# Norm rows from products with ones, smaller first pieces, earlier weight requests and five state buffers in a hybrid recurrent step

## The chip, the cores and the metric

The kernel runs on one core of one Trainium2 chip. A core has a matrix engine (TensorE, PE in the profile; its weight loads are PEld), a vector engine (VectorE, DVE), an engine for functions of one operand (ScalarE, ACT), a general one (GpSimd, POOL) and a queue engine (SyncE, SP) that here only issues transfers. Each engine works through its own instructions in order and waits on semaphores for the others. The metric is the time of one launch in microseconds on the device; lower is better. Kernels are compared by the median of several launches.

## The reference

One step of a two-layer decoder trunk runs over 256 prompt tokens and 8 x 8 sample tokens, 320 rows of 2048 columns, all in float32. Layer 0 mixes a gated delta rule (8 heads of 128x128 state) with gated linear attention (4 heads of 128x256 state); layer 1 is a gated linear recurrence (RG-LRU). What matters here are the norms, the four large products and the states:

```python
def _rmsnorm(x, g):
    xf = x.astype(jnp.float32)
    y = xf * lax.rsqrt(jnp.mean(xf * xf, axis=-1, keepdims=True) + EPS)
    return (y * g.astype(jnp.float32)).astype(x.dtype)

for l in range(DEPTH):                       # DEPTH = 2
    if l % 2 == 0:
        h = _rmsnorm(x, ab_norm[j])
        y, sa, ca, sb = _ab_mixer(h, ...)    # einsum with w_in, conv, delta rule, GLA, einsum with w_out
    else:
        h = _rmsnorm(x, lru_norm[j])
        y, hl, cl = _lru_mixer(h, ...)       # einsum with w_in, conv, gates, scan, einsum with w_out
    x = x + y
return (_rmsnorm(x, final_norm), ...)        # and all new states
```

For the sample tokens every sequence brings its own states (8 x 8 delta matrices, 8 x 4 GLA matrices), which are read, updated and written back.

## The kernel before

**Layout.** Activations lie with the 2048 columns on partitions, 16 tiles of 128 x 320 (tokens on the free axis). A dense product is made in "groups" of 512 output columns, 30 in all: 14 for the input projection of layer 0, 4 for its output, 8 for the input of layer 1, 4 for its output. A group runs over 8 "chunks" of weights (two blocks of 128 x 512, 512 KB). Float32 accuracy comes from splitting both operands into a high and a low part, so each pair of blocks takes three products (line 242): high x high, high weights x low x, low weights x high x. A chunk thus has 2 x 4 x 3 = 24 products of 320 columns, and the kernel has 5760 of them. A group accumulates in four PSUM banks (`accs`, four buffers), so the next group's first product needs the first bank of the group before to have been read.

**Weights.** `load_chunk` (line 197) asks for a chunk on the SP queue into one of three buffers `wst`. `split_chunk` (line 210) makes the high part `wh` on ACT (line 216) and the low part `wl` on DVE (line 219), six half-chunk buffers each. While chunk i is multiplied, chunk i+2 is split (`ahead`, line 224), and at the start of chunk i chunk i+3 is asked for (line 235). The first chunk is special: its halves are asked for by SP and ACT at once (lines 207, 208 and 1599), and the first half is cast on DVE (line 218).

**The order of the rest.** All other work is written as Python generators in three queues, `hi`, `lo` and `tails`. After each half of a chunk's quarter, `slot` advances each queue by one `yield`; there are eight slots per chunk. A table `WAITS` says how many yields a generator lets pass at each place. The framework then orders each engine's instructions by priority (the order in which they are emitted, with offsets for the splits and evictions) and by when their inputs are ready, so an instruction emitted late can run early. `behind` ties one to the product emitted last. When a queue runs late, `finish`, `until` and `drain` empty it on the spot.

**First norm row (r0).** `tables` (line 1658) loads x a second time, with tokens on partitions (`xtok`, 2.6 MB in eight transfers). `start_work` (line 1671) makes the sums of squares from it: two DVE instructions and one ACT instruction for each of four column blocks. `row_rstd` (line 311) scales them, takes the power -1/2 on POOL (line 279), and `spread_rows` (line 303) turns the column into a row on all partitions with three products against the identity (line 307); DVE copies it into `rb0` (line 318). `rb0` multiplies the results of the first layer's groups. Group 0's raw results are put into the buffer `slab` by ACT (lines 421, 422) and scaled later in `taps` (line 430), followed by the convolution (lines 434 to 437). There is one `slab`; group 1's eviction (`evac_padded`, lines 326 and 327) writes into it after group 0's taps have read it and POOL has written the margins (lines 353, 354). Between groups 1 and 2 stands `small_group` (line 461, `smacc`).

**Second norm row (r1).** In `evac_res`, `sumsq` (line 1348) squares each new quarter of x on ACT and adds it up on DVE into `sqa`; at the end five products with one column of ones (lines 1365 to 1367) give the sums by token, and `row_rstd` makes `rb1`.

**States.** `sample_states` (line 909) updates the sample states: for each, a load on SP into one of three buffers (lines 976 and 982, tag `ust`), products, DVE updates (lines 1033, 1047), and a store issued by POOL (lines 1036, 1050). The delta states go beside the output projection of layer 0, the GLA states beside that of layer 1.

**The tail.** In `evac_fin` (line 1535) the last group's results are squared on ACT (line 1541), summed with one column of ones (line 1564, `fsp`), brought to the power -1/2 on POOL (line 1574), spread to a row twice (line 307, `frow`) and multiplied onto the output (lines 1826 to 1832).

Of the kernel before, what the change touches and what calls it, by code (L numbers as in the profile page):

```python
# [30 lines left out]
WARM = 7  # L31
HP = 10
# [34 lines left out]


@with_exitstack
def hybrid_step(ctx, tc, x_cols, x_rows, w_dense, w_small, w_lr, w_gate, par_a, par_b, par_c, gains, head_rows,  # L70
                state_delta, state_gla,
                y_cols, p_delta, p_gla, s_delta, s_gla, dconv, lconv, lru_out):
    nc = tc.nc
# [1822 lines left out]
```

## Time and profile before

| | |
|---|---|
| median of 3 runs | 1004.45 us (1003.6 to 1009.33) |
| the profiled execution | 1000.21 us, of which the span of instructions is 998.4 us |
| mean granted TensorE clock | 0.993 |
| busy PE, DVE, ACT, POOL | 976.0, 722.4, 516.8, 193.4 us |
| transfers | 174.25 MB, mean 175 GB/s |

How to read it: the profile is one execution, and all times in it are microseconds from the first instruction. Matmuls are pipelined, and their shown durations overlap (a product of 320 columns is shown as 0.31 us, while a new one starts about every 0.147 us), so a busy PE isn't yet a PE at its pace; the distance between starts tells more. In a timeline a row gives start, duration, engine (with q: the engine's queue part), line, operation, tiles and count; in brackets stands how long the engine had been idle before it and what ended that. In the chain that ended last a row gives start, length and what ran. In the list of groups a row ends with busy time and mean nanoseconds, then idle time before the group. In the list of waits a row gives who waited for whom, total, times, and the longest.

### The profile page before, as it was taken

To read this page: it belongs to the slowest core of one execution; us is meant where nothing else is said; L and a number is where in the kernel's file an instruction comes from. 1 tells how busy PE (TensorE), PEld (TensorE's weight loads), DVE (VectorE), ACT (ScalarE), POOL (GpSimd) and SP (SyncE) were. 2 spreads that over 40 slices of the span, in tenths; PEclk is the share of its full clock that TensorE was granted. 3 is DMA by queue.
4 is the path that set the end of the run, shared out by engine and by line. 5 is a ranking of instruction groups with operands and counts; after the bars stand their busy time and mean duration, and the time that the engine had idled before them with its cause. 6 is when DMAs were issued, how large, how long until landed. Compare 5 with 4: busy or idle time off the path is not lost.

```text
span 998.4 us, 18969 instructions
## 1 busy us (share of the span) xinstructions
PE 976.0 (98%) x7063; PEld 955.9 (96%) x7063; DVE 722.4 (72%) x1520; ACT 516.8 (52%) x1041; POOL 193.4 (19%) x326
## 2 busy tenths in 40 slices
PE   9999999999999999999999999999999999999995
PEld 8999899999999998899989999999999999999995
DVE  7888887666445456998776789677887776676753
ACT  6567755447323453765233345358778763333441
POOL 4010128302282010201111334100000000054000
PEclk9999999999999999999999999999999999999997
DMA  8853455533555276254786777654554455668742
GB/s 299 284 154 127 130 136 150 167 106 118 114 171 161 86 231 200 66 145 123 236 256 216 246 242 255 222 157 123 161 161 131 146 152 153 182 177 295 272 127 105
DMA packets 64167, 174.25 MB, mean 175 GB/s; under 512 B 16360, under 2 KB 21244, under 8 KB 63564
## 3 DMA queue, kind: packets, MB, share of 16 engines
q1 hardware_dynamic: 58948, 162.71, 52.5%
q0 software_dynamic: 2720, 8.66, 2.4%
q10 hardware_dynamic: 2408, 1.68, 0.5%
q8 instruction: 55, 0.90, 0.4%
q14 instruction: 36, 0.29, 0.1%
HBM read 158.35 MB, written 14.68 MB: 173 GB/s over the span
## 4 chain that ended last, share of the span: by engine, by line
PE 84%; DVE 6%; DMA 5%; issue 2%; ACT 1%; POOL 0%; SPq 0%; DVEq 0%; ACTq 0%; POOLq 0%
PE acc L242 73%; DMA wst<-in_w_dense_dram 4%; DVE wl L219 2%; DMA uvk<-vk_scratch 1%; DVE ob L1831 0%; PE lg L1451 0%; PE lg L1453 0%; PE lg L1452 0%; PE kk L611 0%; PE kq L623 0%; PE gpo L1256 0%; PE po L873 0%; PE y L787 0%; PE gpo L1206 0%; PE sn L1029 0%
## 5 line engine op out<-in xcount | busy, mean ns | idle before, releaser
L242 PE MATMUL acc<-xh,wh 128*128 128x320 f32 x1920 | 600.8, 313 | 6.3 <-ACT wh L216 3.4
L242 PE MATMUL acc<-xh,wl 128*128 128x320 f32 x1920 | 594.1, 310 | 1.7 <-DVE wl L219 1.7
L242 PE MATMUL acc<-xl,wh 128*128 128x320 f32 x1920 | 594.2, 310 | 0.0
L216 ACT ACTIVATE wh<-wst 128x512 fp32r<-128x512 f32 x479 | 279.8, 623 | 341.2 <-PE acc L242 242.0
L219 DVE TENSOR_TENSOR wl<-wst,wh 128x512 fp32r<-128x512 f32 x480 | 333.0, 724 | 152.1 <-ACT wh L216 151.4
L242 PEld LDWEIGHTS acc<-xh,wh 128*128 128x128 f32 x1920 | 360.9, 188 | 9.2 <-ACT wh L216 5.4
L242 PEld LDWEIGHTS acc<-xh,wl 128*128 128x128 f32 x1920 | 360.6, 188 | 2.2 <-DVE wl L219 1.9
L242 PEld LDWEIGHTS acc<-xl,wh 128*128 128x128 f32 x1920 | 361.0, 188 | 1.5 <-issue 0.4
L436 DVE SCALAR_TENSOR_TENSOR yc<-slab,pa,yc 128x344 f32<-128x344 f32 x72 | 42.6, 607 | 1.6 <-ACT yc L99 1.3
L662 POOL TENSOR_TENSOR xi<-xi,tmp 128x60 f32<-128x60 f32 (+24 forms) x62 | 26.7, 431 | 4.9
L718 POOL TENSOR_TENSOR so<-so,mhalf 128x4 f32<-128x4 f32 (+1 forms) x6 | 5.8, 971 | 110.7 <-DVE so L717 100.4
L929 POOL TENSOR_TENSOR uvkh<-uvk,uvkh 32x256 fp32r<-32x256 f32 (+1 forms) x8 | 11.5, 1436 | 73.4 <-DVE uvkh L925 68.8
L660 POOL TENSOR_TENSOR tmp<-ab,xi 128x60 f32<-128x60 f32 (+24 forms) x62 | 24.7, 399 | 4.8
L1480 POOL MEMSET aa<- 128x32 f32 x4 | 0.7, 164 | 116.3 <-ACT rr L1467 82.6
L1033 DVE SCALAR_TENSOR_TENSOR ust<-ust,es,sn 128x128 f32<-128x128 f32 x64 | 17.8, 341 | 5.9 <-PE sn L1029 5.2
L934 POOL TENSOR_TENSOR uvm<-uvh,rm 96x512 fp32r<-96x512 f32 x16 | 21.3, 1358 | 0.3
L1411 DVE SCALAR_TENSOR_TENSOR yc<-slab,pb,yc 128x344 f32<-128x344 f32 x32 | 18.0, 573 | 0.6 <-ACT yc L1409 0.6
L99 ACT ACTIVATE yc<-slab,pa 128x344 f32<-128x344 f32 x24 | 13.6, 577 | 6.5 <-DVE slab L327 4.9
L1036 POOL DMA_DIRECT2D out_s_delta_dram<-ust x8 | 4.6, 578 | 60.4 <-DVE ust L1033 60.4
L1047 DVE SCALAR_TENSOR_TENSOR ugt<-ugt,ebs,gsn 128x256 f32<-128x256 f32 x32 | 14.1, 474 | 3.0 <-PE gsn L1043 3.0
L440 ACT ACTIVATE qkv<-yc 128x256 f32<-128x256 f32 x24 | 9.9, 413 | 11.1 <-DVE yc L436 11.1
L326 DVE TENSOR_TENSOR slab<-acc,rb 128x256 f32<-128x256 f32 x36 | 15.1, 419 | 0.7 <-PE acc L242 0.3
(443 smaller groups left out, 992.7 us busy)
## 6 DMA issues: line engine op xcount, KB each, us to landing
wst<-in_w_dense_dram SPq DMA_DIRECT2D x239, 512.0 KB
st<-in_state_delta_dram SPq DMA_DIRECT2D x8, 512.0 KB
st<-in_state_gla_dram SPq DMA_DIRECT2D x4, 1024.0 KB
ust<-in_state_delta_dram SPq DMA_DIRECT2D x8, 512.0 KB
out_s_delta_dram<-ust POOLq DMA_DIRECT2D x8, 512.0 KB, 4.8
ugt<-in_state_gla_dram SPq DMA_DIRECT2D x8, 512.0 KB
out_s_gla_dram<-ugt POOLq DMA_DIRECT2D x8, 512.0 KB, 6.7
x0r<-in_x_cols_dram SPq DMA_DIRECT2D x8, 320.0 KB
```

The source lines that it names most:

```text
L99: return act.activation(out, in_, AF.Identity, scale=scale)
L216: act.activation(h, wst[i][:, a, :], AF.Copy)
L219: env["last_split"] = dve.tensor_sub(l, wst[i][:, a, :], h.bitcast(F32))
L242: mm = pe.matmul(o, (h, h, l)[j][:, fs], (xh, xl, xh)[j][k], start=(k == 0 and j == 0), stop=(k == KT - 1 and j == 2))
L326: dve.tensor_mul(xp[:, 3:259], xp[:, 3:259] if acc is None else acc[:, :256], rb[:, :256])
L436: dve.scalar_tensor_tensor(y[:, :n], xp[:, j:j + n], pa[:, ft, j:j + 1], y[:, :n], op0=OP.mult, op1=OP.add)
L660: behind(pool.tensor_mul(tv, ab[:, j, j + 1:, None].to_broadcast([P, m, w]), xi[:, j:j + 1, :w].to_broadcast([P, m, w])))
L662: behind(pool.tensor_add(xi[:, j + 1:, :w], xi[:, j + 1:, :w], tv))
L934: pool.tensor_mul(m, src.bitcast(F32)[:, None, :].to_broadcast([R, 4, P]), rm4[:R, :, None].to_broadcast([R, 4, P]))
L1033: dve.scalar_tensor_tensor(s_, s_, es[:, col:col + 1], ps[:, b, :], op0=OP.mult, op1=OP.add)
L1047: dve.scalar_tensor_tensor(s_, s_, ebs[:, h, 4 * hb + b + i:4 * hb + b + i + 1], ps[:, i * 256:(i + 1) * 256], op0=OP.mult, op1=OP.add)
L1411: dve.scalar_tensor_tensor(y[:, :n], xp[:, j:j + n], pb[:, ft, 2 + j:3 + j], y[:, :n], op0=OP.mult, op1=OP.add)
```

## The change

The two norm rows are made from sums of squares in the layout that x already has. For r0 ACT squares the four x tiles, POOL adds the 16 parts up, and one product with a full square of ones gives the sum by token on all partitions as a row; ACT adds epsilon and takes the root, DVE the reciprocal, and POOL makes one correcting Newton step. The second load of x is gone. r1 uses the same `row_rstd` on `sqa`. The final row keeps its way, but its sums are 128 columns wide, and two of the last four gains are issued between the last squares. The first chunk is asked for on SP alone, the first half in two pieces of 256 columns, cast by DVE and ACT; the first x tile's successor is asked for between the halves. A tiny ACT instruction stands early, before x has come. From chunk 8 on, chunk i+4 is asked for in the second quarter of chunk i; before that, chunk i+3 at its start. The state buffers are five instead of three. Many entries of `WAITS` differ.

```diff
+NEAR = 8
...
-    "row_rstd.1": 6, "margins.1": 28, "margins.2": 0, "conv_state_out.1": 5, "conv_state_out.2": 0, "later_g.1": 7,
+    "row_rstd.1": 1, "row_rstd.2": 1, "margins.1": 28, "margins.2": 0, "conv_state_out.1": 0,
...
-    "gla.4": 19, "evac_gate_apply.1": 9, "evac_gate_apply.2": 3, "evac_res_sumsq.1": 10, "evac_res_sumsq.2": 22,
-    "evac_res_sumsq.3": 6, "evac_res_sumsq.4": 17, "evac_lru_evac_taps.1": 5, "evac_lru_evac_taps.2": 5,
+    "evac_gate_apply.2": 3, "evac_res_sumsq.1": 4, "evac_res_sumsq.2": 23, "evac_res_sumsq.4": 17,
...
-    "evac_gate2_apply.2": 8, "evac_fin_work.1": 4, "start_work.1": 32, "start_work.2": 8, "start_work.5": 0,
+    "evac_gate2_apply.1": 19, "evac_gate2_apply.2": 8, "evac_fin_work.1": 4, "start_work.1": 0, "start_work.2": 12,
...
-    "sample_states.14": 7, "gla_out.2": 2, "tables.1": 8, "start_work.9": 2, "masks.1": 5, "masks.2": 2,
+    "sample_states.13": 0, "sample_states.14": 7, "gla_out.2": 2, "tables.1": 8, "start_work.9": 15, "masks.1": 5,
...
+    def load_first():
+
+        t = wst[0] = wpool.tile([P, 2, 512], F32, name="wst", tag="wst", bufs=3)
+        for n in (0, 256):
+            sp.dma_start(t[:, 0, n:n + 256], w_dense[0, 0, :, 0, n:n + 256])
+        load_x(sp, 1, 1)
+        sp.dma_start(t[:, 1], w_dense[0, 0, :, 1])
+
+    def split_first():
+        h, l = [wpool.tile([P, 512], F32R, name=n, tag=n, bufs=6) for n in ("wh", "wl")]
+        w = wst[0][:, 0, :]
+        a, b = slice(0, 256), slice(256, 512)
+        dve.tensor_copy(h[:, a], w[:, a])
+        act.activation(h[:, b], w[:, b], AF.Copy)
+        whl[0, 0] = (h, l)
+        return [lambda c=c: dve.tensor_sub(l[:, c], w[:, c], h[:, c].bitcast(F32)) for c in (a, b)]
...
-            load_chunk(i + 3)
+            if i < NEAR:
+                load_chunk(i + 3)
...
+                if f == 1 and i >= NEAR:
+                    for c in range(i + (3 if i == NEAR else 4), i + 5):
+                        load_chunk(c)
...
-    def row_rstd(ws, ss, out, nm):
-
-        dve.tensor_scalar(ss, ss, 1.0 / D, None, op0=OP.mult)
-        rsqrt_small(ss, 3, ws)
+    def row_rstd(v, t, sq, out, nm):
+
+        ps = bank(nm + "ps")
+        behind(pe.matmul(ps[:, :NT], ones, sq, start=True, stop=True))
         yield from wait("row_rstd.1")
-        ps = bank(nm + "ps")
-        spread_rows(ps, ss)
-        dve.tensor_copy(out, ps[:, :NT])
+        act.activation(v, ps[:, :NT], AF.Identity, scale=1.0 / D, bias=eps[:, 0:1])
+        act.activation(out, v, AF.Sqrt)
+        yield from wait("row_rstd.2")
+        dve.reciprocal(out, out)
+        pool.tensor_mul(t, out, out)
+        pool.tensor_mul(t, t, v)
+        pool.tensor_scalar(t, t, -0.5, 1.5, op0=OP.mult, op1=OP.add)
+        pool.tensor_mul(out, out, t)
...
-                    st = ws.tile([P, 8, P], F32, name="ust", tag="ust", bufs=3)
+                    st = ws.tile([P, 8, P], F32, name="ust", tag="ust", bufs=5)
...
             if m == 3:
-                ps = bank("ssp")
...
-                yield from row_rstd(ws, ss, rb1, "r1")
+                yield from row_rstd(sq[:, 0], sq[:, 1], env["sqa"], rb1, "r1")
...
-                fin["last"] = act.activation(sq[:, f, :], x, AF.Square)
+                i = act.activation(sq[:, f, :], x, AF.Square)
                 if f < 2:
                     dve.tensor_add(fin["sqa"], fin["sqa"], sq[:, f, :])
+                else:
+                    with tc.issue_after(i.ins):
+                        gain(f - 2)
+                    if f == 3:
+                        fin["last"] = i
...
-                n = P if c < 2 else 64
-                pe.matmul(fin["ps"][:n, c:c + 1], sq[:, c * P:c * P + n], ones[:, 0:1],
+                a = min(c * P, NT - P)
+                pe.matmul(fin["ps"][:, c, :], sq[:, a:a + P], ones,
                           start=(i == 0 and c == 0), stop=(i == 2), skip_group_check=True)
...
-    load_chunk(0, (sp, act))
-    load_x(sp, 1, 1)
+    load_first()
     load_chunk(1)
...
+    act.activation(start.tile([P, 1], F32, name="table"), mhalf[:, 0:1], AF.Copy)
     warm = bank("warm")
...
     def start_work():
...
+        sums = start.tile([P, 4, NT], F32, name="xsums")
+        for m in range(4):
+            sq = start.tile([P, 4, NT], F32, name="xsq", tag="xsq", bufs=2) if m else sums
+            behind(act.activation(sq, ob[m], AF.Square))
+            yield from wait("start_work.9")
+            for f in range(4 if m else 0):
+                pool.tensor_add(sums[:, f], sums[:, f], sq[:, f])
+        for f in range(1, 4):
+            pool.tensor_add(sums[:, 0], sums[:, 0], sums[:, f])
         yield from wait("start_work.2")
-        yield from row_rstd(start, s3, rb0, "r0")
+        yield from row_rstd(sums[:, 1], sums[:, 2], sums[:, 0], rb0, "r0")
```

The removed part of `start_work` is the loop over `xtok` described above, and `tables` loses its four `rows` entries.

More of the change, by code (lines that the diff above doesn't have):

```diff
@@ L371, in hybrid_step @@
     start = start_p.__enter__()
-    xtok = [start.tile([P, 3, 512], F32, name="xtok", tag="xtok", bufs=4) for _ in range(4)]
     smw = start.tile([P, KT, 32], F32, name="smw")
@@ L981, in state_in @@
                 hb, h = r % 2, 2 * u + r // 2
[L982 removed]
+                st = ws.tile([P, 4, 256], F32, name="ugt", tag="ust", bufs=5)
                 behind(sp.dma_start(st, state_gla[h, :, 4 * hb:4 * hb + 4, :]))
@@ L1362, in sumsq @@
             if m == 3:
-                ps = bank("ssp")
-                sqa = env["sqa"]
-                for c in range(2):
-                    pe.matmul(ps[:, c:c + 1], sqa[:, c * P:(c + 1) * P], ones[:, 0:1], start=True, stop=True)
-                pe.matmul(ps[:64, 2:3], sqa[:, 256:320], ones[:, 0:1], start=True, stop=True)
-                ss = ws.tile([P, 3], F32, name="ss1", tag="ss1")
-                dve.memset(ss, 1.0)
-                dve.tensor_copy(ss[:, 0:2], ps[:, 0:2])
-                dve.tensor_copy(ss[:64, 2:3], ps[:64, 2:3])
-                yield from wait("evac_res_sumsq.3")
-                yield from row_rstd(ws, ss, rb1, "r1")
+                yield from row_rstd(sq[:, 0], sq[:, 1], env["sqa"], rb1, "r1")
                 env["done"].add("r1")
@@ L1578, in last @@
             with tc.issue_after(fin["last"].ins):
-                for f in range(4):
-                    scaled(ob[3][:, f, :], ob[3][:, f, :], pb[:, 12 + f, 42:43])
+                for f in (2, 3):
+                    gain(f)
             yield
@@ L1697, in start_work @@
         yield from wait("start_work.5")
+    lows = split_first()
     x_tile(0)
-    split_chunk(0, 0)
+    for fn in lows:
+        fn()
     with tc.issue_after(env["xs"][0].ins):
```

49 lines of the change are left out of this document (12 added, 37 removed), and 33 rows, old and new, of the table WAITS.

## The prediction

> **What bounds the kernel now.** I read the page first, then busy time by stretches of the span, then the chain that ended last, and then the timelines of the start, of the first norm row and of the state stage.
>
> ```profile
> PE 976.0 (98%) x7063; PEld 955.9 (96%) x7063; DVE 722.4 (72%) x1520; ACT 516.8 (52%) x1041; POOL 193.4 (19%) x326
> PE acc L242 73%; DMA wst<-in_w_dense_dram 4%; DVE wl L219 2%; DMA uvk<-vk_scratch 1%; DVE ob L1831 0%; PE lg L1451 0%; PE lg L1453 0%; PE lg L1452 0%; PE kk L611 0%; PE kq L623 0%; PE gpo L1256 0%; PE po L873 0%; PE y L787 0%; PE gpo L1206 0%; PE sn L1029 0%
> ```
> ```profile
> 8.90:875.00 866.10, 859.77 (x6297) 841.12 (x6295) 642.94 (x1383) 468.88 (x959) 159.49 (x285) 1.00 0.55 170
> 25.00:50.00 25.00, 25.00 (x174) 25.00 (x174) 20.94 (x68) 13.19 (x34) 1.67 (x3) 1.00 0.89 283
> 100.00:125.00 25.00, 23.08 (x160) 22.43 (x159) 20.60 (x47) 19.07 (x61) 3.74 (x6) 1.00 0.41 129
> 875.00:925.00 50.00, 46.64 (x320) 46.18 (x319) 37.16 (x59) 18.18 (x31) 23.83 (x20) 1.00 0.77 242
> 984.87:990.00 5.13, 3.22 (x15) 2.94 (x15) 2.10 (x6) 1.19 (x3) 0.96 (x2) 0.50 0.09 33
> ```
> (A row of the second block: the stretch and its length, then the busy time of PE, PEld, DVE, ACT and POOL, the granted clock, the DMA share, GB/s.) TensorE is the bound, and nothing in the change takes dense products away. So only time in which PE stands still or runs slowly can be won: from 8.90 to 875 us that is 866.10 - 859.77 = 6.3 us, in the last state stage (875 to 925) 50.00 - 46.64 = 3.4 us, and beside these the start and the tail. A gain of 1% (10 us, about what a measurement of this kernel can tell from no change) would need most of all of it.
>
> **The start: first weights in two pieces, ACT's table ahead.**
>
> ```profile
> 0.74 0.39 SPq L377 DMA_DIRECT2D ob<-in_x_cols_dram  x1
> 1.06 3.35 PE L1619 MATMUL warm<-ones 128*128 128x128 f32 x14 [1.06 <-DVE xss L1676]
> 3.16 1.28 ACT L99 ACT_TABLE_LOAD   x1 [3.16 <-DMA ob<-in_x_cols_dram]
> 4.46 0.56 ACT L99 ACTIVATE xh<-ob,gcol 128x320 fp32r<-128x320 f32 x1
> 4.81 0.75 DVE L218 CAST wh<-wst 128x512 fp32r<-128x512 f32 x1 [3.47 <-DMA wst<-in_w_dense_dram]
> 5.70 1.40 PE L242 MATMUL acc<-xh,wh 128*128 128x320 f32 x4 [1.29 <-DVE wh L218]
> 7.52 1.15 ACT L216 ACTIVATE wh<-wst 128x512 fp32r<-128x512 f32 x2 [0.93 <-DMA wst<-in_w_dense_dram]
> 8.90 0.31 PE L242 MATMUL acc<-xh,wh 128*128 128x320 f32 x1
> ```
> ```profile
> 1.18 3.60 DMA wst<-in_w_dense_dram
> 12.27 33.98 PE acc L242 x231
> 46.26 0.61 PE r0ps L307 x6
> 65.41 2.29 PE smacc L461 x32
> 87.81 0.64 PE sml L1106 x2
> ```
> PE waits from the end of the warm products (1.06 + 3.35 = 4.41) to 5.70 for the first half of the weights, which lands 3.60 us after its issue while the other half comes at once, and then for a cast of 0.75. Its first twelve products then take 8.90 - 5.70 = 3.20, against 12 x 33.98/231 = 1.77 at the later pace. Afterwards the first x piece (160 KB), a first weight piece (128 KB) and a second stand on one queue, 0.44 apart (0.74 to 1.18). The x piece took 3.16 - 0.74 = 2.42 from its issue; with the same for the pieces, they land at 1.18 + 2.42 = 3.60 and about 4.05. The table load is over long before, so xh is ready at 3.16 + 0.56 = 3.7. DVE casts the first piece (half of 0.75) to 4.0, ACT the second to about 4.4. If PE waits for the whole tile it starts at 4.4, a gain of 1.3. Bounds: 0 (the pieces take the 3.60 of the old half plus 0.44) to 1.6. The pace comes on top. A start without the 1.29 pause should shorten the slow stretch; its loss is 3.20 - 1.77 = 1.4, between none and all of it comes back, and I take 0.5, because chunk 1 is now asked for after five other transfers and is hardly earlier than its 7.52. Start: **-1.8** (0 to -2.4, as the second chunk's data end the rest).
>
> The Trainium skill ("TensorE: Matmul & The Clock Gate", Part 1) says that the array starts at half clock and is let up after one busy window of some 3.4 us, with windows that run free of the program. By that rule the gap-free start can come up to speed anywhere between about 4.5 and 7.9 us, an estimate from that page, and the term would be -1.3 to -2.4; the trace's slow twelve products agree with it.
>
> **The first norm row (r0).** Out go the 2.6 MB of x rows with eight SP issues, eight DVE passes, four ACT squares, the POOL power and six small products. In come four ACT squares of 128x1280, 15 POOL additions of 128x320, one product with ones, and a chain up to rb0. The additions cost 15 x 0.77 = 11.5 us (0.77 is half of the 128x640 row below); they lie in a stretch where POOL is busy 1.67 of 25 us, before 45 us, and DVE, which they may slow, has just lost its eight passes there. Cost 0. Were that cover gone, the product would wait for POOL, 11.5 at most. The chain itself is longer:
>
> ```profile
> L1827 POOL TENSOR_TENSOR ob<-ob,frows 128x640 f32<-128x640 f32 x1 | 1.5, 1537 | 3.4 <-ACT frows L1826 3.4
> L1454 ACT ACTIVATE rr<-lg,pb 128x320 f32<-128x320 f32 x16 | 8.4, 528 | 2.1 <-PE lg L1453 2.0
> ```
> ```profile
> L583 DVE RECIPROCAL nb<-ss 128x4 f32<-128x4 f32 x5 | 0.9, 179 | 3.3 <-POOL ss L571 3.2
> L286 DVE RECIPROCAL spas<-spas 128x20 f32<-128x20 f32 x1 | 0.3, 278 | 0.0
> ```
> ```profile
> 47.19 0.48 DVE L318 COPY rb<-r0ps 128x320 f32<-128x320 f32 x1
> 47.71 0.43 DVE L326 TENSOR_TENSOR slab<-slab,rb 128x256 f32<-128x256 f32 x1
> 48.19 1.29 DVE L219 TENSOR_TENSOR wl<-wst,wh 128x512 fp32r<-128x512 f32 x2
> 60.59 0.57 DVE L436 SCALAR_TENSOR_TENSOR yc<-slab,pa,yc 128x344 f32<-128x344 f32 x1
> 62.80 0.42 DVE L326 TENSOR_TENSOR slab<-acc,rb 128x256 f32<-128x256 f32 x1
> ```
> ```profile
> 61.34 0.28 POOL L354 COPY slab<-pa 128x96 f32<-128x96 f32 x1
> ```
> By the yields before it, the product is emitted in call 88 of its queue instead of call 86, two slots of 24 x 0.147 / 8 = 0.44 later: 46.26 + 0.88 = 47.14. Then: two records 0.64, the step to the reader 0.32 (46.87 to 47.19), Identity 0.53, a table load for Sqrt 1.28, Sqrt 0.53, the reciprocal (16 more elements cost 99 ns, so 179 + 316 x 6.2 ns = 2.1 us), four POOL passes of 0.77 (3.1), and one pair of wh on ACT ahead of them 1.15. rb0 is ready at 56.8 where it was at 47.67: 9.1 later. POOL, DVE and ACT have room for it; the reader does not. The taps of group 0 fill DVE from 47.71 to 61.16, 13.5 us with eight splits of 0.6 (48.19, two in 1.29) and 0.5 of small work between. The one slab is then free, POOL writes its margin by 61.62 (0.46 after the taps), and group 1's first eviction reads its bank from 62.80 on (0.42 for 256 of the 320 columns, so about 0.5). PE needs that bank only after smacc, at 67.70. In the changed kernel DVE is nearly idle until 56.8 and has its splits done; with five splits instead of eight and no small work between, the taps end at 56.8 + 13.5 - 0.5 - 1.8 = 68.0, margin and eviction make 69.0, and PE waits **+1.3**. Bounds: 0 (more splits put off) to 6.1 (no relief, 61.16 + 9.1 + 1.0 = 71.2, which is 3.5, and 2.6 if each of the four POOL passes waits for a split). I take the value near the low end, since the DVE rows it is counted from are those of the same work.
>
> **The second norm row (r1).** Its row comes 44 yields after the square before and 27 + 1 + 1 after; the product is 17 slots (7.5 us) earlier and the longer chain eats that. Its first reader comes 5.7 us after the row was ready, so a late row costs nothing:
>
> ```profile
> 642.88 0.49 DVE L318 COPY rb<-r1ps 128x320 f32<-128x320 f32 x1 [1.44 <-PE r1ps L307]
> 649.07 0.42 DVE L326 TENSOR_TENSOR slab<-acc,rb 128x256 f32<-128x256 f32 x1
> ```
> On PE six one-column records (0.13 each by the fsp row below) and six of a row (0.61) give way to two (0.64): -0.75. For r0 0.61 gives way to 0.64, nothing.
>
> **Weights asked for ahead, five state buffers.**
>
> ```profile
> SPq L205 <- DVE wl L219: 568.5, 197, 16.4
> SPq L983 <- DMA out_s_gla_dram<-ugt: 12.5, 3, 6.3
> ```
> ```profile
> 896.25 10.15 DMA wst<-in_w_dense_dram
> 913.03 10.15 DMA wst<-in_w_dense_dram
> ```
> Of 239 weight loads 197 stand in SP until the split frees their buffer. The three weight buffers stay three, so asking earlier moves none of these, only the few behind other requests. The state buffers do remove the 12.5 us in which SP stood before a state load until a store had landed; queued behind it were weight loads. But the two stalls of this stage follow loads that took 10.15 us from issue to landing, in a queue full of states and stores, and the same bytes still pass. I take **-1.0** of the 3.4 (bounds -3.4 to +1.5, if states that come earlier delay weights more). What is late next is the split behind the load. What SP now holds behind an earlier weight request (states, scratch reads) is itself waited for half a chunk later at the earliest: 0.
>
> **Tail and waits.**
>
> ```profile
> 982.88 2.40 PE fsp L1564 x18
> 986.54 1.56 PE frow L307 x6
> ```
> The 18 one-column records become 128 columns wide; at full clock that is about the same 0.13 each. The row's six records took 1.56 at a granted clock of 0.50 and 0.61 for r0: 0.95 to win if wider products hold the clock, -0.6 to lose if they run cold. I take **-0.5**, with one DVE instruction fewer in it. Two gains of ob move ahead of the last squares; nobody waits for them before the row is there: 0. The retimed yields move work by a few slots under PE: 0, between -2 and +2 by the 1.9 us that PE stands idle from 100 to 125.
>
> **The sum.** -1.8 + 1.3 - 0.75 - 1.0 - 0.5 = -2.75 us. The profiled execution took 1000.21 us (998.4 in the span, 1.8 around it) and would take 997.5; the median of the three runs, 1004.45, is 0.4% above it, and 1004.45 - 2.75 gives **1001.7**.
>
> **Rivals.** *rb0 comes later still, and the kernel ends slower.* One mechanism: POOL's four passes and DVE's splits hold each other up. For it speaks a split pair beside a POOL pass:
>
> ```profile
> 918.90 2.48 POOL L934 TENSOR_TENSOR uvm<-uvkh,rm 96x512 fp32r<-96x512 f32 x2
> 918.94 2.99 DVE L219 TENSOR_TENSOR wl<-wst,wh 128x512 fp32r<-128x512 f32 x2 [2.44 <-ACT wh L216]
> ```
> 2.99 for two instead of 1.29. Four waits of 0.65 put rb0 at 59.4; a split beside them loses 0.85, some 1.0 in all, and PE's wait at 67.70 becomes 1.3 + 2.6 + 1.0 = 4.9. DVE carries that into the next late stretch, where PE's 1.9 us idle double: -4.05 + 4.9 + 1.9 = +2.75, so 1007.2. It decides where PE's wait passes the 4.05 won elsewhere, with rb0 at about 59; slower by 1% needs rb0 near 68. Against it: DVE has little to do while it waits for rb0. The Trainium skill ("SBUF — State Buffer", "Who interferes with whom") says that a DVE instruction with two SBUF inputs and a GpSimd one that reads SBUF exclude each other, the later waiting for the whole of the other; by that rule the first chain above is too short by these waits, and the row just shown agrees.
>
> *Asking ahead hides nothing:* the 197 waits speak for it; then the 1.0 is gone, 1002.7.
>
> *Faster by over 1%:* the new order empties the queues. All of 6.3 + 3.4, with 2.4 at the start, 0.75 and 0.95, is 13.8; three quarters are 10.4, so 994. Against it stands that most of these idle times follow no step that is changed.
>
> **Chances.** Forecast 0.58, rb0 still later 0.17, nothing hidden 0.13, large gain 0.12. The range 995.5 to 1007 leaves out the outer part of the gain and of the late row, under 2 in 10. Faster by over 1% (below 994.4) 0.09, within 1% 0.86, slower (above 1014.5) 0.05.
>
> **What would show it.** First dense product near 4.4; rb0 written about 9 us after its product's old place, and a PE gap after smacc; no SP wait on state stores; stalls in the last state stage about two thirds as long; the six frow records at 0.1 each. Wrong would be: no gap after smacc, or one of over 4 us; weight loads landing in 5 us; the dense product still at 5.7.

## The result: slower by 0.9%, and the profile after

| | median us | runs | span and clock of the profiled execution |
|---|---|---|---|
| before | 1003.60 | 999.64 to 1009.33 | 998.4, 0.993 |
| changed | 1012.75 | 1008.15 to 1016.19 | 1014.3, 0.990 |

One further run of the kernel before, at 1188.83 us, is left out of its range as slow. The ratio of changed to before is 1.0087, 95% interval 1.0067 to 1.0107: 9 us lost where 2.75 were to be won. That is still within 1%, the case that had been given most of the chance, but outside the range of 995.5 to 1007. The profiled execution of the changed kernel (1016.19 with what lies around its span) is the slowest of its runs; its distance to the one before, 16 us, is more than the 9 us between the medians.

Lines of the changed kernel's file stand 16 to 20 further down (the dense product is L259, the splits L234 and L235, row_rstd L327 to L339). First the same table of busy time by stretches as before (stretch and length, busy PE, PEld, DVE, ACT, POOL, granted clock, DMA share, GB/s), shifted by 15 us where the stages are late:

```profile
8.90:890.00 881.10, 864.07 (x6294) 843.21 (x6293) 652.54 (x1366) 476.13 (x964) 179.66 (x305) 1.00 0.54 165
25.00:50.00 25.00, 23.82 (x161) 23.40 (x160) 21.80 (x46) 14.47 (x33) 14.81 (x16) 1.00 0.56 177
890.00:940.00 50.00, 45.73 (x300) 44.78 (x299) 31.68 (x54) 17.93 (x31) 22.32 (x20) 0.97 0.76 239
```

TensorE stands still for 17.0 us in the long middle, where it was 6.3, and for 4.3 in the last state stage, where it was 3.4. From 25 to 50 us there was no idle time and is now 1.2; POOL's 1.67 became 14.81. The last row's clock of 0.97 is new.

Where along the kernel the time went is seen from the start of a chunk's first dense product, counted in the two traces (us; changed kernel minus before):

```
chunk        0      1      8     16     24     48     64     96    120    208    232
before    5.70  10.66  36.41  67.63  99.85 194.74 275.19 430.23 533.42 862.24 954.46
changed  -1.62  +0.09  +1.63  +3.49  +4.61  +4.38  +7.04 +12.55 +12.13 +12.04 +16.75
```

The profiled execution of the kernel before is quicker than its median by 3 us, so the late distances in this table are some 3 to 4 us too large: u_row0 below, whose times equal those of the kernel before, stands 4.35 behind it at chunk 232 in its profile.

**The head** does what was said, and gives it back. The timeline of TensorE after:

```profile
4.08 1.58 PE L259 MATMUL acc<-xh,wh 128*128 128x320 f32 x4
5.50 0.75 PE L259 MATMUL acc<-xl,wh 128*128 128x320 f32 x4
6.08 0.75 PE L259 MATMUL acc<-xh,wl 128*128 128x320 f32 x4
7.87 0.42 PE L259 MATMUL acc<-xh,wh 128*128 128x320 f32 x1 [1.03 <-ACT wh L234]
10.75 0.71 PE L259 MATMUL acc<-xh,wh 128*128 128x320 f32 x3 [0.86 <-ACT xh L100]
```

The first product stands at 4.08, and at full clock from 5 us on the first twelve are over at 6.83, in 2.75 us where they took 3.20. Then TensorE waits 1.03 for the second half of the first weights, now asked for behind an x tile, and 0.86 for chunk 1, which starts at 10.75 where it was 10.66. (ACT splits the weights of chunk 1 from 9.10 on, when they have landed, and only then makes the xh that TensorE waits for.)

**The first norm row** costs in two places. Between 23 and 31 us POOL adds squares while DVE splits (timelines of POOL, DVE and TensorE after):

```profile
23.19 4.33 POOL L1696 TENSOR_TENSOR xsums<-xsums,xsq 128x320 f32<-128x320 f32 x4 [5.52 <-ACT xsq L1693]
...
23.60 1.91 DVE L1327 SCALAR_TENSOR_TENSOR xl<-ob,gcol,xh 128x320 fp32r<-128x320 f32 x2 [0.92 <-ACT xh L100]
25.43 3.24 DVE L235 TENSOR_TENSOR wl<-wst,wh 128x512 fp32r<-128x512 f32 x3
...
28.12 0.42 PE L259 MATMUL acc<-xh,wl 128*128 128x320 f32 x1 [1.18 <-DVE wl L235]
```

An addition takes 1.08 us in this group, not 0.77, and three splits take 3.24, where three together take 1.9 without additions (shown below). TensorE then waits 1.18 for the split. Then the row itself:

```profile
49.35 0.53 ACT L332 ACTIVATE xsums<-r0ps,eps 128x320 f32<-128x320 f32 x1
49.89 1.28 ACT L333 ACT_TABLE_LOAD   x1
51.18 0.47 ACT L333 ACTIVATE rb<-xsums 128x320 f32<-128x320 f32 x1
...
51.14 1.29 DVE L235 TENSOR_TENSOR wl<-wst,wh 128x512 fp32r<-128x512 f32 x2
52.35 0.69 DVE L1701 TENSOR_TENSOR smw<-smw,gcol 128x512 f32<-128x512 f32 x1
52.96 2.15 DVE L335 RECIPROCAL rb<-rb 128x320 f32<-128x320 f32 x1
...
55.18 1.04 POOL L336 TENSOR_TENSOR xsums<-rb 128x320 f32<-128x320 f32 x1 [9.77 <-DVE rb L335]
56.30 1.21 POOL L337 TENSOR_TENSOR xsums<-xsums 128x320 f32<-128x320 f32 x1
57.60 0.46 POOL L338 TENSOR_SCALAR xsums<-xsums 128x320 f32<-128x320 f32 x1
58.14 0.88 POOL L339 TENSOR_TENSOR rb<-rb,xsums 128x320 f32<-128x320 f32 x1
...
69.75 0.11 POOL L374 MEMSET slab<- 128x12 f32 x1 [10.73 <-ACT smpQ L462]
...
71.11 0.39 PE L259 MATMUL acc<-xh,wh 128*128 128x320 f32 x1 [1.17 <-DVE slab L348]
74.01 0.63 PE L492 MATMUL smt<-quart,sm 128*128 128x32 f32 x4 [0.90 <-DVE sm L483]
```

rb0 is ready at 59.02 (it was 47.67), the taps of group 0 end and the slab's margin is written at 69.75, and TensorE waits 1.17 after the small products and 0.90 more for their result.

**The clock.** Three times before the tail, a stretch of exactly one 3.41 us window runs at half clock. Two of these stand right behind a window in which TensorE stood still for over 2 us:

```profile
424.74:428.16 3.42, 1.32 (x6) 0.85 (x6) 3.42 (x6) 2.77 (x8) 0.40 (x3) 1.00 0.00 0
428.16:431.57 3.41, 3.41 (x11) 3.06 (x11) 2.71 (x6) 0.72 (x4) 1.47 (x4) 0.50 0.22 55
...
936.74:940.16 3.42, 0.54 (x4) 0.46 (x4) 2.27 (x5) 2.30 (x4) 0.78 (x1) 1.00 0.61 200
940.16:943.57 3.41, 3.41 (x15) 3.41 (x14) 3.41 (x9) 1.94 (x3) 0.33 (x1) 0.50 0.54 155
```

The first column after the length is PE's busy time: 1.32 of 3.42 (idle 2.10), then a window at 0.50. The second of the two half-clock windows has 15 products, where a window of dense products at full clock has 25 or 26. Such a window loses half its length, 1.7 us, beside the stall. The third, from 902.61 on, follows a window that is shown idle for only 1.39 us:

```profile
899.20:902.61 3.41, 2.02 (x11) 1.30 (x10) 3.14 (x3) 3.06 (x6) 2.50 (x3) 1.00 0.04 14
```

The kernel before has no half-clock window between 8.65 and 984.86 us.

### The profile page after: what moved, and what is told of

It is laid out like the page before. It is cut to its first block, busy times and chain, and to the rows that moved or that the text cites. A ratio compares the mean times of both kernels' runs of the same rounds, so it can differ in the third digit from the quotient of the medians.

```text
span 1014.3 us, 18944 instructions
## 1 busy us (share of the span) xinstructions
PE 979.8 (97%) x7049; PEld 956.7 (94%) x7049; DVE 726.5 (72%) x1497; ACT 523.1 (52%) x1045; POOL 212.4 (21%) x345
## 5 line engine op out<-in xcount | busy, mean ns | idle before, releaser
L259 PE MATMUL acc<-xh,wh 128*128 128x320 f32 x1920 | 601.8, 314 | 8.5 <-ACT wh L234 3.9
L259 PE MATMUL acc<-xh,wl 128*128 128x320 f32 x1920 | 595.4, 311 | 4.9 <-DVE wl L235 4.9
L259 PE MATMUL acc<-xl,wh 128*128 128x320 f32 x1920 | 595.3, 310 | 0.0
L234 ACT ACTIVATE wh<-wst 128x512 fp32r<-128x512 f32 x479 | 278.5, 623 | 346.1 <-PE acc L259 247.5
L235 DVE TENSOR_TENSOR wl<-wst,wh 128x512 fp32r<-128x512 f32 x479 | 336.4, 735 | 143.6 <-ACT wh L234 142.5
L259 PEld LDWEIGHTS acc<-xh,wh 128*128 128x128 f32 x1920 | 362.0, 189 | 12.2 <-ACT wh L234 9.0
L259 PEld LDWEIGHTS acc<-xh,wl 128*128 128x128 f32 x1920 | 361.5, 189 | 6.6 <-DVE wl L235 6.3
L259 PEld LDWEIGHTS acc<-xl,wh 128*128 128x128 f32 x1920 | 362.0, 189 | 1.2
L456 DVE SCALAR_TENSOR_TENSOR yc<-slab,pa,yc 128x344 f32<-128x344 f32 x72 | 40.1, 576 | 2.5 <-ACT yc L100 2.2
L460 ACT ACTIVATE qkv<-yc 128x256 f32<-128x256 f32 x24 | 9.9, 414 | 12.2 <-DVE yc L456 12.2
```

The costliest lines, as they stand in the source:

```text
L234: act.activation(h, wst[i][:, a, :], AF.Copy)
L235: env["last_split"] = dve.tensor_sub(l, wst[i][:, a, :], h.bitcast(F32))
L259: mm = pe.matmul(o, (h, h, l)[j][:, fs], (xh, xl, xh)[j][k], start=(k == 0 and j == 0), stop=(k == KT - 1 and j == 2))
L456: dve.scalar_tensor_tensor(y[:, :n], xp[:, j:j + n], pa[:, ft, j:j + 1], y[:, :n], op0=OP.mult, op1=OP.add)
```

## The experiments

Theory "row": the new first norm row is what costs, by the additions and by being late, and its stalls set off others. Rivals: "order", the retimed yields; "requests", the weights asked for ahead; "chain", rb0's longer chain. Each kernel ran in several rounds beside the kernel before. "Full-clock time" is the median over the runs of time times mean granted clock; "half clock" is the mean of the rest, that is half of all stretches at a clock of 0.50. In every kernel the rest holds the end, where TensorE has little left to do: in the profiles 5.1 to 7.0 us with the old tail (before, b_row0, row0_again, stall_a, stall_b) and 2.9 to 4.7 with the new one. So these two columns compare only kernels that have the same tail. Clocks are listed to 0.001, 1 us of a run. The ratio compares runs of the same round; where it and the medians differ, the text goes by the ratio (0.001 is 1 us).

| kernel | median us | before beside it | ratio, 95% interval | full-clock | half clock |
|---|---|---|---|---|---|
| before (beside the u_ kernels) | 1004.16 | | | 997.1 | 7.3 |
| changed | 1012.75 | 1003.60 | 1.0087 (1.0067 to 1.0107) | 1004.6 | 8.6 |
| u_row0 | 1003.75 | 1004.16 | 0.9994 (0.9973 to 1.0014) | 997.8 | 6.2 |
| u_head | 1011.24 | 1004.16 | 1.0050 (1.0028 to 1.0073) | 1003.1 | 7.4 |
| u_ask | 1012.24 | 1004.16 | 1.0070 (1.0048 to 1.0092) | 1003.9 | 7.8 |
| u_waits | 1009.17 | 1004.16 | 1.0039 (1.0021 to 1.0057) | 1002.2 | 6.9 |
| v_noadds | 1009.19 | 1005.30 | 1.0042 (1.0021 to 1.0063) | 1002.0 | 7.2 |
| v_early | 1012.25 | 1005.30 | 1.0072 (1.0049 to 1.0096) | 1005.0 | 7.9 |
| v_both | 1006.06 | 1003.17 | 1.0030 (1.0014 to 1.0046) | 1000.0 | 5.9 |
| b_row0 | 1012.67 | 1005.30 | 1.0059 (1.0037 to 1.0082) | 1000.7 | 11.4 |
| row0_again | 1010.11 | 1004.32 | 1.0052 (1.0032 to 1.0072) | 1000.2 | 10.1 |
| r0w | 1004.43 | 1005.30 | 0.9997 (0.9980 to 1.0014) | 998.0 | 6.6 |
| keep | 1003.30 | 1003.17 | 1.0004 (0.9986 to 1.0022) | 996.9 | 6.1 |
| r1_tail | 1003.97 | 1004.32 | 1.0001 (0.9981 to 1.0022) | 999.8 | 4.4 |
| stall_a | 1013.64 | 1003.17 | 1.0122 (1.0099 to 1.0144) | 1008.2 | 6.7 |
| stall_b | 1031.39 | 1003.17 | 1.0291 (1.0264 to 1.0318) | 1021.3 | 11.0 |

### One part of the change undone

u_row0 takes r0 from the x rows again, with its own yields as before:

```diff
-        sums = start.tile([P, 4, NT], F32, name="xsums")
-        for m in range(4):
...
+        for cc_ in range(4):
+            for c in range(3):
+                behind(dve.scalar_tensor_tensor(j[:n], x_, 1.0, x_, op0=OP.mult, op1=OP.mult,
+                                                accum_out=ss[:n, c, cc_:cc_ + 1]))
...
+        yield from rstd_old(start, s3, rb0, "r0")
```

> The changed kernel with the first norm row taken from the token-major rows again, as before; all else as changed. Theory 'row': the 1.45 us stall in the seventh chunk (weight splits held up by POOL's additions and ACT's squares), the 1.17 us after the small products and the 0.90 us after it all come from the new row, so the first product of group 2 stands within 1 us of its old place and the median falls by 4 to 6 us, to 1007 to 1009. Rival 'order' (the retimed yields) or 'requests' (weights asked for half a chunk later): the early stalls go as well, but the stalls from 270 us on stay and the median stays above 1008. If late work early on is what sets off the later stalls, the whole 9 us go: below 1005.

It went below the first theory's band, to 1003.75, and from a ratio of 1.0087 to 0.9994: the whole loss goes with the row, the third case. TensorE's middle has 11.0 us of idle time, where the changed kernel had 17.0 and the kernel before 6.3:

```profile
8.90:880.00 871.10, 860.13 (x6275) 838.62 (x6274) 645.46 (x1379) 469.68 (x962) 160.44 (x287) 1.00 0.55 170
```

Of the 12.4 us between the two profiles at chunk 232, 2.6 lie before chunk 24. From chunk 28 on TensorE's other work stands at the same dense products in both, so the later part is not a new order on TensorE; it is the same waits grown longer (at the first product of chunk 64, 282 us: 2.42 of idle time against 0.64, and 1.38 in the kernel before; at 398 us: 1.82 against 0.79) and three half-clock windows, 5.1 us, against none.

u_head:

```diff
-    load_first()
+    load_chunk(0, (sp, act))
+    load_x(sp, 1, 1)
...
-    for fn in lows:
-        fn()
+    split_chunk(0, 0)
```

> The changed kernel with the first weights loaded and split as before (two halves on two queues, no early table load). The first product should come near 5.7 again instead of 4.1. Theory 'given back': the second chunk starts at 10.7 in both forms, so the time stays within 1 us of the changed kernel's 1012.75. Rival: the pieces shift later loads, and undoing them wins or loses over 2 us.

1.5 us lower by the median, 3.7 by the ratio, with intervals that just touch: not "within 1 us"; if anything, the rival. The first product is at 5.72, chunk 1 at its old place, and the stall of the seventh chunk is gone: chunk 8 stands 0.20 behind the kernel before instead of 1.63. In the seventh chunk the additions stall TensorE only together with the new head: in b_row0 and row0_again below, which have them without it, chunk 8 stands within 0.2 us of its old place.

u_ask:

```diff
-            if i < NEAR:
-                load_chunk(i + 3)
+            load_chunk(i + 3)
...
-                if f == 1 and i >= NEAR:
-                    for c in range(i + (3 if i == NEAR else 4), i + 5):
-                        load_chunk(c)
```

> The changed kernel with each weight chunk asked for at the start of a chunk, three ahead, as before. Theory 'requests': SP stands longer with a request whose buffer is still in use, and reads behind it come late (the 1.8 us wait for the transposed state block at 396 us, the 2.4 us wait for weights at 280 us); undone, these stalls shrink below 1 us and the median falls by 3 to 6 us, to 1007 to 1010. Theories 'row' and 'order': within 1.5 us of 1012.75.

0.5 us by the median, 1.7 by the ratio, inside the intervals: "requests" falls. In its profile the wait at 280 us is 2.29, nearly as long as in the changed kernel. The other wait named, 1.82 for the transposed block, did shrink, to 0.73, without a gain that the intervals can tell.

u_waits sets the 24 other entries of `WAITS` that differ back ("fill.2": 14 to 9, "gla_out.1": 6 to 8 and so on).

> The changed kernel with the yields of all work but the two norm rows set as before (24 of the table's entries). Theory 'order': the stalls at 396, 402, 411, 425 and 426 us (5.4 us) come from helpers that now stand elsewhere; undone, they shrink to the 1.5 us of before and the median falls by 4 to 8 us, to 1005 to 1009. Theories 'row' and 'requests': within 2 us of 1012.75, either side.

3.6 us lower by the median, just short of the band of "order" and outside that of its rivals; 4.8 by the ratio, and the intervals don't meet. The stalls of 1.39 and 0.71 at 425 us are gone, as expected; the second norm row's product, whose yields stayed, then waits 1.91 for its sums at 640 us.

### The row's two stalls, and the row alone

v_noadds drops the 15 `pool.tensor_add`; v_early changes one number, `"start_work.9": 15` to 10; v_both does both. b_row0 is the kernel before with the new row alone, r0w the changed kernel with old row and all old yields.

> The changed kernel without the 15 additions on POOL that sum the squares for the first norm row; the row is then taken from the first square alone, so a part of the computation is left out. Theory 'additions': they hold up DVE's weight splits; without them the 1.45 us stall in the seventh chunk goes (ninth chunk at 36.6 instead of 38.05) and most of the row's 9 us with it, 1004 to 1006. Theory 'late row': only that stall goes; the row itself is as late as before, the 2.5 us of stalls between 64 and 74 us and what follows stay, 1009 to 1012.

> The changed kernel with the first norm row's squares 10 slots apart instead of 15, so its product stands 20 slots (8.8 us) earlier and the row is ready near 50 us instead of 59. Theory 'late row': the stalls of 0.48, 1.17 and 0.90 us between 64 and 74 us go, later ones with them; the median falls by 4 to 8 us, to 1005 to 1009. Theory 'additions': the additions are crowded into less time, the stall of the seventh chunk grows by up to 2 us, and the median stays within 2 us of 1012.75.

v_noadds came out between the two, at the lower end of "late row": 4.5 us below the changed kernel by the ratio, half of the row's cost. DVE is back to its pace (timeline of DVE):

```profile
24.05 1.90 DVE L235 TENSOR_TENSOR wl<-wst,wh 128x512 fp32r<-128x512 f32 x3 [0.49 <-ACT wh L234]
25.87 1.01 DVE L1327 SCALAR_TENSOR_TENSOR xl<-ob,gcol,xh 128x320 fp32r<-128x320 f32 x2
```

Three splits take 1.90 instead of 3.24, the pair of xl 1.01 instead of 1.91, and chunk 8 starts at 36.14. The wait after the small products shrinks to 0.66 but stays, the 0.90 too.

v_early did not gain beyond the intervals (1.5 us by the ratio, 0.5 by the median), and its profile shows why. All three stalls between 64 and 74 us are gone, and others stand in their place (timelines of POOL, ACT and TensorE, then TensorE's windows):

```profile
25.39 9.77 POOL L1787 TENSOR_TENSOR xsums<-xsums,xsq 128x320 f32<-128x320 f32 x8 [0.98 <-ACT xsq L1784]
...
38.66 0.22 ACT L604 ACTIVATE al<-al 128x20 f32<-128x20 f32 x1 [4.34 <-DVE al L595]
...
39.33 0.42 PE L350 MATMUL acc<-xh,wh 128*128 128x320 f32 x1 [2.08 <-ACT slab L533]
```
```profile
36.48:39.89 3.41, 1.32 (x10) 1.06 (x9) 3.34 (x8) 1.00 (x5) 2.00 (x4) 1.00 0.59 203
39.89:43.30 3.41, 3.41 (x14) 3.04 (x12) 2.71 (x14) 2.24 (x8) 0.00 (x0) 0.50 0.64 144
```

Eight additions stand back to back, and DVE falls behind. ACT waits 4.34 for a small result of DVE's, and group 0's eviction, which is ACT's next work, comes late by that. TensorE waits 2.08 for the eviction, beside 1.16 for a split at 27 us, and the window after the longer wait runs at half clock.

> The changed kernel with both steps at once: no additions on POOL (the row from the first square alone, so a part of the computation is left out) and the squares 10 slots apart. Theory 'two stalls': the additions and the late row each stall TensorE by themselves, moving the row earlier failed only because the additions were crowded; with both gone nothing is left of the row's cost and the time is that with the old row, 1002 to 1006. Rival 'chain': the chain itself (reciprocal on DVE, table load and square root on ACT, four POOL passes) or the missing transfers cost as well: 1008 or more.

1006.06 lies at the edge of "two stalls" and below "chain". By the ratios moving the row, once the additions are gone, brings 1.2 us more (1.0042 to 1.0030), less than the intervals can tell, and 3.6 us remain against u_row0. So the two stalls aren't shown to be all of it: v_both still has the four squares on ACT and the longer chain, and lacks the second load of x. Its profile has the same 2.1 us of waits at 419 us, here within one window (half clock from 422.02 on), and one of 2.47 at 928 us with half clock behind it; which step of the row leads there stays open.

> The kernel before with the new first norm row alone (its squares, additions, chain and its own yields). If the row costs its 9 us by itself: 1011 to 1014. If it costs the local 4 us alone and the rest comes from its meeting the other edits: 1006 to 1009.

> The changed kernel with both the first norm row and all yields as before; the second row, the head, the earlier requests, the five state buffers and the tail stay as changed. If the two costs add (9.0 for the row, 3.6 for the yields): 1000 to 1001.5, below the kernel before. If the yields were only late because of the row: 1003 to 1005.

By its median b_row0 is in the band "by itself", by its ratio it costs 6 us; it was run again, below. The row is enough to make the kernel slower, with neither the new head nor the other new yields. r0w is where the second case had it, 1003 to 1005: the yields' cost exists only together with the new row. What ties them wasn't found; the wait at 425 us comes with the new yields in all kernels that have them (1.39 and 0.71 us in u_row0 too, without a half-clock window behind them).

### What a stall costs

The row alone once more, for its clocks:

> The same kernel as the one before with the new first norm row alone, once more, for a second profile and more times. Its first profile lost 4.1 us by the 24th chunk and 6.4 us in all, its median 7.4. Theory 'clock windows': the rest comes in runs in which a stall leaves more than about 1.85 us of one 3.41 us window idle; then this profile has one or more windows at half clock behind stalls (at 62 to 72, 109, 278 or 928 us), the mean granted clock over the runs is lower than in the runs of the kernel before, and time times clock is only 3 to 4 us above it. Theory 'all stalls': time times clock is 7 us above it and the clocks are alike. The median again 1010 to 1014.

The windows of this second profile:

```profile
107.43:110.84 3.41, 1.58 (x11) 1.32 (x10) 3.41 (x7) 2.08 (x3) 0.00 (x0) 1.00 0.04 12
110.84:114.25 3.41, 3.41 (x14) 3.41 (x14) 3.41 (x8) 0.57 (x2) 0.00 (x0) 0.50 0.59 156
...
278.09:281.51 3.42, 1.41 (x10) 1.18 (x9) 3.42 (x9) 2.07 (x4) 2.93 (x7) 1.00 0.30 97
281.51:284.92 3.41, 3.41 (x15) 3.41 (x14) 2.19 (x6) 0.00 (x0) 2.86 (x8) 0.50 0.72 232
```

"Clock windows" holds: there are two half-clock windows, at two of the places named, and in the table 3.5 us of full-clock time (1000.2 against 996.7 of the runs of before beside it) and 2.7 of half clock. In b_row0, whose profile has no such window, the runs together show 3.3 and 3.4. The window at 107 us had a stall before the change too, just a shorter one (windows of the kernel before):

```profile
104.23:107.64 3.41, 1.75 (x12) 1.49 (x11) 3.41 (x7) 1.69 (x2) 0.00 (x0) 1.00 0.21 30
107.64:111.05 3.41, 3.41 (x25) 3.41 (x24) 3.41 (x7) 1.67 (x5) 0.00 (x0) 1.00 0.64 189
```

1.66 us idle and the next window at full clock; 1.83 idle, and it runs at half. To have this by itself, stall_a and stall_b put ten pauses into quiet chunks of the kernel before:

```diff
+                if f == 2 and 164 <= i < 204 and i % 4 == 2:
+                    ps = bank("hold")
+                    pe.matmul(ps[:, :P], ones, ones, start=True, stop=True)
+                    act.activation(hold[:, :P], ps[:, :P], AF.Copy)
+                    for _ in range(3):
+                        pool.tensor_add(hold[:, :320], hold[:, :320], hold[:, :320])
+                    pe.matmul(ps[:, P:2 * P], ones, hold[:, :P], start=True, stop=True)
```

(stall_a: one addition of 256 columns.)

> The kernel before with ten made pauses of TensorE, one every fourth chunk from 166 to 202 (a small product, a copy on ACT, one POOL addition of 256 columns, a product of its result), each some 1.2 to 1.6 us. Theory 'half window': idle time costs its own length as long as no 3.41 us window is more than about half idle (1.85 us); the time rises by the sum of the pauses, 12 to 16 us, and the granted clock stays. Theory 'length only' expects the same here; the comparison is with the next run.

> The same with three POOL additions of 320 columns, each pause some 2.7 to 3.3 us. Theory 'length only': the time rises by the sum of the pauses, 27 to 33 us. Theory 'half window': a pause of 3 us leaves over 1.85 us idle in one window in about 8 of 10 phases, and the window after it runs at half clock, 1.7 us each: 13 us more, 40 to 46 us, with some eight windows at a granted clock of 0.50 in the profile.

The pauses came out shorter than meant: single waits of 0.3 to 1.4 in stall_a, of 1.2 to 2.5 in stall_b. The times rose by 12.2 and 29.2 us by the ratios. As written, "half window" missed for stall_b: it named 40 to 46 us and some eight windows, and the profile has four; 29.2 lies in the band of "length only", but that band too was written for longer pauses. So the sums decide nothing, and the clocks and the windows must: half clock is 6.7 in stall_a, as in the kernel before (6.8), and 11.0 in stall_b. Windows of stall_b:

```profile
708.26:711.67 3.41, 1.58 (x12) 1.32 (x11) 1.82 (x2) 3.39 (x6) 3.11 (x5) 1.00 0.53 191
711.67:715.08 3.41, 3.41 (x15) 3.41 (x15) 2.23 (x5) 0.68 (x2) 0.00 (x0) 0.50 0.63 162
...
800.42:803.83 3.41, 1.84 (x14) 1.58 (x12) 2.19 (x3) 3.09 (x6) 2.57 (x3) 1.00 0.48 144
803.83:807.24 3.41, 3.12 (x22) 3.12 (x23) 2.79 (x3) 0.89 (x2) 0.24 (x1) 1.00 0.53 154
```

1.83 idle is followed by half clock, 1.57 is not, although the pause at 802.26 to 804.12 was 1.86 long: it lay across the edge of two windows, at 803.83.

### The parts that were to gain, alone

keep is the kernel before with the head, r1 and the tail; r1_tail the same without the head.

> The kernel before with the head, the second norm row and the tail of the change, and nothing else of it (old first row, yields, requests, three state buffers). By the positions in the profiles the head gives 1.0, the second row 0.75 and the tail 1.1: 2 to 3 us below the kernel before. Rival: these gains are lost again at the later waits for weights: within 1 us of it.

> The kernel before with the second norm row and the tail of the change alone: no new head, no new first row, no new yields, requests or buffers. The second row gives 0.75 us of TensorE time and the tail some 1.1: 1.5 to 2 us below the kernel before, if nothing takes them back. The head should then have cost what the run with all three parts lacked, 2 us. If this is within 0.5 us of the kernel before, the gains are lost at later waits.

Neither shows a gain: 1.0004 and 1.0001. The rivals hold by the medians. The intervals (down to 0.9986 and 0.9981) rule out the 2 to 3 us that were expected of keep, but not quite the 1.5 to 2 of r1_tail. The single gains are there in the profiles (r1_tail's chunks 144 to 152 take 0.81 less, 28.76 instead of 29.57, and from the last dense product to the end it is 14.8 instead of 15.9), but keep waits 1.73 for chunk 1 at 9.16 and has a half-clock window from 13.28 on, and both lose 1.5 between chunks 152 and 208. So do r0w and u_waits: the loss stands in the profiles of the four kernels that have the new second row with the old yields, and in no other profile without made pauses. Only 0.3 of it is a wait on the list, so what it is stays open. None of these kernels beats the kernel before beyond its interval.

## Why the prediction was wrong

- **The first norm row**, "+1.3", is the step that failed. At the place where it was costed, its mechanism was right: rb0 at 59.0 for 56.8, the wait after the small products 1.17 for 1.3. That the wait met its figure is in part luck: rb0 was 2.2 us later than forecast, and TensorE came to the wait 2.2 later too (69.94, where the small products had ended at 67.70), held up by its earlier stalls. And the row was costed at that one place. The row alone shifts chunk 24 by 4.1 and 3.75 us in its two profiles (waits of 1.49 and 0.84 for splits at 63 us and 1.88 after smacc in each), and by its ratios costs 5 to 6 us; in the whole change its undoing gives back 9.
- **"The additions ... Cost 0"** was wrong in its size and its cover. Counted at 0.77 each, they took 0.94 to 1.17 in the changed kernel (1.22 in v_early's eight) and stretched the DVE splits beside them by 70%; without them 4.5 of the row's 9 us are gone. The reason given, that DVE "has just lost its eight passes there", fails on time: these passes stood at 28.35 us and later, and the splits that TensorE waits for are worked on from 25.43. The Trainium skill ("SBUF — State Buffer", "Who interferes with whom") was cited for the four passes of the chain; it bore on the additions too, and there the trace agrees in direction: one addition and one split took the same 1.08 us each, where a split alone takes 0.63. It doesn't show that one waits for the whole of the other: 0.63 and the 0.77 counted would make 1.40.
- **The start**, -1.8: 1.62 at the first product, and 0 at chunk 1. The bound was the second chunk's data and the work on them, as the prediction's bracket had said without taking it as the value.
- **r1**, -0.75: seen as -0.81 in r1_tail between chunks 144 and 152, and lost again later; in the changed kernel the same chunks gain 0.37. **Tail**, -0.5: the end after the last dense product went from 15.9 to 15.1 in the profiled execution. The sums take 2.3 us, where they took 2.4. The wider products held the clock, which fell at 1005.01, after the row, where it had fallen at 984.86, before it. So the twelve records of the row's two spreads take 1.55 instead of 2.83, 0.13 each for the 0.1 given:

```profile
999.63 0.94 PE L1583 MATMUL fsp<-ones,fsqa 128*128 128x128 f32 x6
1000.40 1.50 PE L1583 MATMUL fsp<-ones,slab 128*128 128x128 f32 x12
1003.13 1.55 PE L323 MATMUL frow<-ident,fr 128*128 128x128 f32 x12 [1.23 <-POOL fr L1592]
```

- **Weights and state buffers**, -1.0: nothing. SP no longer waits for state stores, as said, and the stalls of the last state stage grew (4.3 for 3.4) all the same; on the chain that ended last, two loads there take 11.49 and 10.48 us from issue to landing, where it was 10.15. Asking earlier leaves as many loads waiting for their buffer as before (200, where it was 197):

```profile
SPq L207 <- DVE wl L235: 600.3, 200, 19.0
```

- **Waits**, 0 (within 2): the retimed yields cost 3.6 to 4.8 us with the new row, and none is seen without it.
- **What was missing**: a price for a stall beyond its length. The clock stood in the sum only for the start and the tail. Of the row's cost alone (b_row0 and row0_again), about half is half clock; in the changed kernel's profile the three windows are 5.1 us.
- Of the rivals, the slower one named the right pair of engines, and its point of decision, rb0 at about 59, was met, but in good part by luck. It gave 2.6 us to four waits of the POOL passes; these passes took 3.84 for 3.1, 0.7 more. The larger part is the reciprocal: the root is there at 51.65, but DVE still has two splits and smw before it and starts it at 52.96. And TensorE's wait after the small products, put at 4.9 by this rival, was 1.17. It too left out the additions and the clock.

## What to carry to other kernels

Work moved to an idle engine isn't free where it slows the engine that feeds TensorE, as POOL's additions did with DVE's splits (0.63 to 1.08 us each): look at what the feeding engine is doing in those very microseconds, not at its load over the stretch. A chain that is late by 11 us at one reader should be followed to every reader behind it, since the work that it delays is the same that splits the next weights. And on a kernel bound by TensorE, idle time that comes in one piece of about 2 us can cost twice: where a stall lies inside one window, cutting it from 1.9 to 1.6 us would by these counts save more than its 0.3.

## What was not expected of the hardware

In these traces TensorE's clock falls to half for one window of 3.41 us after a window in which TensorE is shown idle for more than about 1.85 us, far short of a full window. Counted over all sixteen profiles of this case, without the fall in each tail: of the windows with more than 1 us idle, 16 of 16 with over 1.85 were followed by half clock, 3 of 5 between 1.80 and 1.85, and 3 of 76 below that. Shown busy time isn't quite what counts: two of these last three windows (in keep and v_both, in the first 13 us) hold nine or ten products of one column. The fall in the tail of the kernel before, at 984.86, follows a window that is shown busy nearly throughout, 16 of whose products are one column wide:

```profile
981.45:984.86 3.41, 3.31 (x26) 2.99 (x24) 1.86 (x5) 2.46 (x6) 0.00 (x0) 1.00 0.00 0
```

What exactly the clock goes by isn't shown here. The half-clock stretches of the changed kernel's profile stand whole multiples of 3.41 apart (428.16, 902.61 and 940.16: 139 and 11 windows), so it is chance whether a given stall falls into one window or across two, and the clocks listed for the runs of the changed kernel go from 0.989 to 0.995, 6 us of a run. The Trainium skill ("TensorE: Matmul & The Clock Gate", "What's actually happening") has this free-running window of 3413 ns, and the traces agree; its rule in "HAM oscillation — how this bites in real kernels", no idle gaps over about 3.4 us, is too mild here, where 1.83 was enough.
